# A two-layer decoder trunk on one core: the first layer's normed tokens made from a transposed load instead of from rows and transposes

## The chip, the cores and the metric

The kernel runs on one core of a Trainium2 chip. The metric is device time in microseconds for one execution. A core has engines that run side by side and meet at semaphores: TensorE (PE, with its weight loads shown as PEld), VectorE (DVE), ScalarE (ACT), GpSimd (POOL) and SyncE (SP), whose queue issues nearly all DMAs here. Each engine takes its instructions in the order in which the program holds them, so an instruction that waits holds up everything behind it on that engine.

## The reference

`x` is (1, 512, 1024), `mem` is (1, 256, 1024), all in float32. Cut to what matters:

```python
def rmsnorm(x, g):
    return x * lax.rsqrt(jnp.mean(x * x, axis=-1, keepdims=True) + EPS) * g

def reference(x, mem, norm_g, fox_w_in, fox_b_f, ret_w_in, mem_norm_g, w_mem_kv, w_out, final_norm_g):
    mem_n = rmsnorm(mem, mem_norm_g)
    for i in range(2):
        h = rmsnorm(x, norm_g[i])
        proj = h @ (fox_w_in if i == 0 else ret_w_in)[0]     # q, k, v, (forget logits,) q_mem, z
        main = fox_attention(...) if i == 0 else retention(...)       # 12 heads of 128
        memo = mem_cross_attention(q_mem, mem_n, w_mem_kv[i])         # 4 heads of 128
        x = x + (jnp.concatenate([main, memo], -1) * jax.nn.silu(z)) @ w_out[i]
    return rmsnorm(x, final_norm_g)
```

## The kernel before

Every product is made of three products of fp32r halves: an operand is split into a high part (`H`, a ScalarE cast) and a low part (`L`, the rest, by VectorE), and TensorE adds up H·H, H·L and L·H. Weights come in pieces of 128x1024 (512 KB). A piece is loaded by SP into one of four `raw` buffers, ScalarE casts it to `wH` (L136), VectorE makes `wL` (L137), and there are four buffers of each. When TensorE has used a piece up, `retire` splits the next loaded one and, behind its `wL`, `load_piece` (L118) asks for another. So ScalarE's cast of piece n waits until TensorE is done with piece n-4, and the load of piece n until `wL` of piece n-4 is written.

TensorE's order is written out by hand: `cycle(...)` takes a list of fillers (the projections, which use up pieces) and jobs (norms, attention steps), whose steps are hung between fillers at offsets from the table `OFF`. The orders of VectorE, ScalarE, GpSimd and SP are left to a scheduler that goes by priorities (`due`), except for the first splits, whose own order is fixed.

The program begins so:

- `start_mem` loads the transposed memory `memT` and the first pieces. A VectorE memset of `warm` (L900, a `dd` buffer) is followed on TensorE by 13 products on it (L904), ahead of any that counts.
- Cycle one: `f_vm` (memory values of layer 1, pieces 1 to 4, 48 products of 512 columns; L437, L450), `spread` of the memory's factors (L183), `f_km` four times (memory keys of layer 1, pieces 5 to 8, 24 products of 256 columns each; L60). After each key block VectorE scales the sums (L417), ScalarE casts them and VectorE makes the low part.
- Cycle two: `f_km` four times for layer 0 (pieces 9 to 12), `f_vm` for layer 0 (pieces 13 to 16). Between them hang the four `norm` jobs of layer 0: ScalarE squares a block of 128 rows of x (L192), GpSimd makes the factor (L193, L194), VectorE multiplies by factor and `norm_g` (L195), TensorE transposes it in eight products with the identity (L202), and ScalarE and VectorE split the result into `hH` and `hL` (L157, L158).
- Then layer 0's `f_v` on `hH` and `hL` (pieces 17 and 18, L60 with 268 columns), and all the rest.

Of the kernel before, what the change touches and what calls it, by code (L numbers as in the profile page):

```python
# [16 lines left out]
D = 1024  # L17
S = 512
NMEM = 256
EPS = 1e-6  # L20
# [7 lines left out]
PBASE = 1000  # L28
SPAN5 = 17
SPAN5F = 16  # L30
WARM = 13
MAXK = 1.4
WT = 1088


@with_exitstack
def tile_hybrid(ctx, tc, x_in, mem_in, memT_in, g_cols, norm_g, fin_g, b_f, wv0, wp, index, consts, cosT, sinT, dec, out):
    nc = tc.nc
    P = 128
    KD = D // P  # L40
# [10 lines left out]
    def ps_at(kind, shape, dt, name):  # L51
        tag = TAGS[kind]
        return psum.tile(shape, dt, name=name, tag=tag, bufs=BUFS[tag])
# [21 lines left out]
    def tile_(tag, shape, dt=F32):  # L75
        return work.tile(shape, dt, name=tag, bufs=BUFS[tag])

    csb = cst.tile([P, P], F32, name="csb")
    gc = cst.tile([P, KD], F32, name="gc")
    rbm = cst.tile([P, NMEM], F32, name="rbm")  # L80
    ident = csb[:, 0:P]
    nhalf = cst.tile([P, 1], F32, name="nhalf")
    G.memset(nhalf, -0.5)
    eps_t = cst.tile([P, 1], F32, name="eps_t")
# [14 lines left out]
    def load_g(ap):  # L99
        return load(ap.partition_broadcast(P))  # L100
# [62 lines left out]
    def split_new(tag, src, scale=None):  # L163
        H, L = tile_(tag, [P, 512], F32R), tile_(tag, [P, 512], F32R)
        split_to(H, L, src, scale)
        return H, L
# [236 lines left out]
    def f_km(l, h):  # L403
        key = (l, "km", h)

        def fn():
            H, L = pieces[key]
            mT = st["mT"]
            ps = acc_tile()
            terms = []  # L410
            for w, c in ((H, 0), (H, 1), (L, 0)):
                for k in range(KD):
                    terms.append((w[:, k * P:(k + 1) * P], mT[k][c]))
            mm_group(ps[:, :NMEM], terms)
            kt = tile_("km" if l == 0 else "qk", [P, 2, NMEM], F32R)
            kn = tile_("dd", [P, 512])
            V.tensor_tensor(out=kn[:, :NMEM], in0=ps[:, :NMEM], in1=rbm, op=ALU.mult)  # L417
            split_to(kt[:, 0, :], kt[:, 1, :], kn[:, :NMEM])
            st[l, "km", h] = kt
            retire(key)  # L420
        return [([key], fn)]
# [255 lines left out]
    def g_forget():  # L677
# [44 lines left out]
        forget=(0, 2, 3),  # L722
        norm=(0, 2),
        memr=(0, 2.4),
        xload=(0, 1, 2, 3, 4),
    )
    GEN = dict(mem=g_mem, fox=g_fox, ret=g_ret, retn=g_ret, ret2=g_ret, forget=g_forget, norm=norm_gen, memr=lambda: memr_gen(), xload=lambda: xload_gen())

    cycles = []
    tail_jobs = []  # L730
# [12 lines left out]
    def start_mem():  # L743
        nc.scalar.dma_start(out=gc, in_=g_cols)
        src = [tile_("vv", [P, 4, NMEM]) for _ in range(2)]
        rows = [tile_("vv", [P, D]) for _ in range(2)]
        nc.sync.dma_start(out=src[0], in_=memT_in[0])
        load_piece()
        nc.sync.dma_start(out=src[1], in_=memT_in[1])
        for _ in range(BUFS["raw"] - 1):  # L750
            load_piece()
        nc.sync.dma_start(out=csb, in_=consts[:, 0:P])
        for b in range(2):
            nc.sync.dma_start(out=rows[b], in_=mem_in[b * P:(b + 1) * P, :])
        st["msrc"], st["mrows"] = src, rows
        mT = [[tile_("gg", [P, 2, NMEM], F32R) for _ in range(2)] for _ in range(4)]
        st["mTt"] = mT
        st["mT"] = [(m[0][:, k, :], m[1][:, k, :]) for m in mT for k in range(2)]
# [12 lines left out]
        prep_piece(ends)  # L771

    def memr_gen():
        st["mr"] = [rstd_of(st["mrows"][b], st["mrows"][b], f"mr{b}") for b in range(2)]
        yield
        spread(st["mr"], rbm)
        yield

    def xload_gen():
        st["g", 0] = load_g(norm_g[0])  # L780
        yield
        for t in range(NT):
            nc.sync.dma_start(out=xt[t], in_=x_in[t * P:(t + 1) * P, :])
            yield
    def build_layer(l):
        late = []
        M = "fox" if l == 0 else "ret"
# [11 lines left out]
        for pr in range(6):  # L799
# [26 lines left out]


    cycle(f_vm(1, [[(i, 0), (i, 1)] for i in range(4)], first=True) +
          sum([f_km(1, h) for h in range(4)], []), [("memr", (), 1.5), ("xload", (), 0.5)], mode=8)
    cycle(sum([f_km(0, h) for h in range(4)], []) + f_vm(0, [[(i, 0), (i, 1)] for i in range(4)]),  # L830
          [("norm", (t, ("g", 0)), 2.0 * t) for t in range(NT)], start="x", mode=9)
    build_layer(0)

    cycle(f_out_last(0, (5,), lambda *a: None), [("norm", (t, ("g", 1)), t + 0.5) for t in range(NT)],
# [60 lines left out]
    def emit():  # L895
        lead = ExitStack()
        lead.enter_context(tc.manual_schedule(engines={mybir.EngineType.SP}))
        start_mem()
        warm = tile_("dd", [P, 512], F32R)
        V.memset(warm.bitcast(F32), 0.0)  # L900
        A.activation(small.tile([P, 1], F32, name="ss"), eps_t, AF.Copy, scale=1.0)
        wps = acc_tile()
        for i in range(WARM):
            PE.matmul(wps, lhsT=warm[:, :P], rhs=warm, start=(i == 0), stop=(i == WARM - 1))  # L904
        with tc.manual_schedule(engines={mybir.EngineType.DVE, mybir.EngineType.Pool, mybir.EngineType.Activation}):
            for i in range(4):
                if i:
                    mem_split(2 * i)
                    mem_split(2 * i + 1)
                    prep_piece()  # L910
                else:
                    first_splits()
        carry = []
        for ci, (fillers, jobs, start, mode, last) in enumerate(cycles):
            if start == ("lead", 0):
                spill()
                lead.close()
                tro = tile_("dd", [P, 2 * P])
                tc.keep_in_program_order(nc.sync.dma_start(out=tro, in_=consts[:, P:3 * P]))
                tc.keep_in_program_order(A.copy(out=tri, in_=tro[:, :P]))  # L920
                tc.keep_in_program_order(A.copy(out=ones, in_=tro[:, P:]))
                nc.sync.dma_start(out=bfb, in_=b_f.partition_broadcast(P))
            elif start == "l1":
                st["g", 1] = load_g(norm_g[1])
            elif start == "end":
                st["g", 2] = load_g(fin_g)
                end.enter_context(tc.manual_schedule(engines={mybir.EngineType.DVE, mybir.EngineType.Pool, mybir.EngineType.Activation}))
            elif start == ("lead", 1):
                km_load()
            elif start == ("mem", 1):  # L930
                vm_load()
            nF = len(fillers)
            ev = []
            for kind, args, base in jobs:
                box = {}

                def step(kind=kind, args=args, box=box):
                    if "g" not in box:
                        box["g"] = GEN[kind](*args)
                    with due(now[0] + PRIO[0]):  # L940
                        next(box["g"])
                for off in OFF[kind]:
                    ev.append([base + off, step])
            if ev:
                k = min(MAXK, nF / (mode or max(p for p, _ in ev) + 1))
                for e in ev:
                    e[0] *= k
            if start == "l1":
                ev.append([nF + 1.2, flush_retired])
            ev = sorted(carry + ev, key=lambda e: e[0])  # L950
            for c in range(nF):
                with due(now[0] + PRIO[1]):
                    fillers[c][1]()
                now[0] += 1
                while ev and ev[0][0] < c + 1:
                    ev.pop(0)[1]()
            carry = []
            if last:
                tail_jobs.extend(e[1] for e in ev[-1:])
                for e in ev[:-1]:  # L960
                    e[1]()
            else:
                carry = [[p - nF, f] for p, f in ev]

    end = ExitStack()
    tri = cst.tile([P, P], F32R, name="tri")
    ones = cst.tile([P, P], F32R, name="ones")
    bfb = cst.tile([P, 12], F32, name="bfb")
    engines = {"PE": mybir.EngineType.PE, "ACT": mybir.EngineType.Activation, "DVE": mybir.EngineType.DVE,
               "POOL": mybir.EngineType.Pool}  # L970
# [98 lines left out]
```

## Time and profile before

| | us |
|---|---|
| median of three runs (925.40 to 925.78) | 925.57 |
| the profiled execution itself | 925.52 |
| its span, from the first instruction to the last | 923.7 |

The span is what the views of the profile cover; 1.82 us of the profiled execution lie around it. Busy time of an engine says how much of the span it was at work; of a busy TensorE the ends are modelled, so the start times of its instructions tell more than its share.

### The profile page before, as it was taken

To read this page: it belongs to the slowest core of one execution; us is meant where nothing else is said; L and a number is where in the kernel's file an instruction comes from. 1 tells how busy PE (TensorE), PEld (TensorE's weight loads), DVE (VectorE), ACT (ScalarE), POOL (GpSimd) and SP (SyncE) were. 2 spreads that over 40 slices of the span, in tenths; PEclk is the share of its full clock that TensorE was granted. 3 is DMA by queue.
4 is the path that set the end of the run, shared out by engine and by line. 5 is a ranking of instruction groups with operands and counts; after the bars stand their busy time and mean duration, and the time that the engine had idled before them with its cause. 6 is when DMAs were issued, how large, how long until landed. Compare 5 with 4: busy or idle time off the path is not lost.

```text
span 923.7 us, 12322 instructions
## 1 busy us (share of the span) xinstructions
PE 914.7 (99%) x4623; PEld 778.0 (84%) x4623; DVE 593.5 (64%) x1060; ACT 437.2 (47%) x767; POOL 33.6 (4%) x91
## 2 busy tenths in 40 slices
PE   9999999999999999999999999999999999999997
PEld 7998888888888888888898898888888888888985
DVE  6866664553755564645557756576678675888865
ACT  6744453332544233433325444454457464676642
POOL 0100100000000000000000010000000000000001
PEclk9999999999999999999999999999999999999999
DMA  9774322222332221423223152323323321632302
GB/s 337 265 258 142 116 92 92 90 71 69 127 101 81 78 94 53 144 78 103 81 95 100 46 160 70 109 73 95 111 87 119 114 81 58 182 103 81 115 1 91
DMA packets 32195, 100.69 MB, mean 109 GB/s; under 512 B 4348, under 2 KB 4860, under 8 KB 32136
## 3 DMA queue, kind: packets, MB, share of 16 engines
q1 hardware_dynamic: 30984, 97.55, 32.5%
q0 software_dynamic: 864, 2.10, 0.8%
q8 instruction: 36, 0.59, 0.3%
q10 hardware_dynamic: 288, 0.27, 0.1%
q14 instruction: 23, 0.19, 0.1%
HBM read 92.53 MB, written 4.22 MB: 105 GB/s over the span
## 4 chain that ended last, share of the span: by engine, by line
PE 98%; DMA 1%; issue 0%; DVE 0%; ACT 0%; SPq 0%; POOLq 0%; DVEq 0%; POOL 0%; ACTq 0%
PE acc L226 45%; PE acc L60 23%; PE acc L322 10%; PE s L60 6%; PE o L560 5%; PE acc L379 2%; PE acc L450 2%; PE pt L594 1%; PE o L60 1%; PE acc L385 1%; PE pt L529 1%; PE pt L202 1%; DMA raw<-in_wp_dram 1%; DVE wL L137 0%; ACT wH L136 0%
## 5 line engine op out<-in xcount | busy, mean ns | idle before, releaser
L137 DVE TENSOR_TENSOR wL<-raw,wH 128x1024 fp32r<-128x1024 f32 x148 | 180.8, 1224 | 103.9 <-ACT wH L136 64.0
L136 ACT CAST wH<-raw 128x1024 fp32r<-128x1024 f32 (+1 forms) x147 | 153.5, 1049 | 69.8 <-PE acc L226 34.8
L226 PE MATMUL acc<-hL,wH 128*128 128x512 f32 x608 | 163.6, 394 | 0.0
L226 PE MATMUL acc<-hH,wH 128*128 128x512 f32 x608 | 153.5, 394 | 0.0
L226 PE MATMUL acc<-hH,wL 128*128 128x512 f32 x608 | 150.6, 390 | 0.0
L60 PE MATMUL acc<-wH,gg 128*128 128x512 f32 x416 | 135.8, 393 | 0.0
L226 PEld LDWEIGHTS acc<-hH,wL 128*128 128x128 f32 x608 | 114.1, 188 | 24.5
L226 PEld LDWEIGHTS acc<-hH,wH 128*128 128x128 f32 x608 | 111.0, 188 | 21.3
L226 PEld LDWEIGHTS acc<-hL,wH 128*128 128x128 f32 x608 | 111.3, 188 | 20.6
L60 PEld LDWEIGHTS acc<-wH,gg 128*128 128x128 f32 x416 | 78.1, 188 | 15.6
L60 PE MATMUL acc<-wL,gg 128*128 128x512 f32 x208 | 81.1, 390 | 0.0
L342 DVE TENSOR_TENSOR x<-acc,x 128x512 f32<-128x512 f32 (+1 forms) x73 | 49.7, 681 | 38.2 <-PE acc L60 31.1
L157 ACT CAST pTH<-pt 128x128 fp32r<-128x128 f32 (+2 forms) x64 | 29.8, 467 | 63.2 <-PE pt L594 50.6
L584 ACT ACTIVATE p<-dd,nm 128x128 f32<-128x128 f32 (+3 forms) x48 | 27.0, 563 | 68.0 <-DVE nm L580 67.8
L60 PE MATMUL s<-qk 128*128 128x256 f32 (+3 forms) x240 | 53.5, 326 | 0.0
L322 PE MATMUL acc<-wH,hH 128*128 128x512 f32 x128 | 50.4, 394 | 0.0
L322 PE MATMUL acc<-wH,hL 128*128 128x512 f32 x128 | 49.9, 390 | 0.0
L158 DVE TENSOR_TENSOR pTL<-pt,pTH 128x128 fp32r<-128x128 f32 (+2 forms) x64 | 34.2, 536 | 24.3 <-ACT pTH L157 24.1
L322 PE MATMUL acc<-wL,hH 128*128 128x512 f32 x128 | 49.9, 390 | 0.0
L560 PE MATMUL o<-pTH,vv 128*128 128x512 f32 (+1 forms) x192 | 48.4, 314 | 0.0
L157 ACT CAST gg<-sz 128x512 fp32r<-128x512 f32 x28 | 17.4, 622 | 60.9 <-DVE sz L495 39.9
L60 PEld LDWEIGHTS s<-qk 128*128 128x128 f32 x240 | 40.3, 189 | 6.4 <-DVE p L634 0.3
(197 smaller groups left out, 1354.9 us busy)
## 6 DMA issues: line engine op xcount, KB each, us to landing
raw<-in_wp_dram SPq DMA_DIRECT2D x146, 512.0 KB, 3.6
cbc<-c_d SPq DMA_DIRECT2D x12, 256.0 KB, 3.4
cbc<-in_dec_dram SPq DMA_DIRECT2D x12, 256.0 KB, 3.2
dd<-dd SPq DMA_DIRECT2D x48, 64.0 KB, 2.0
x<-in_x_dram SPq DMA_DIRECT2D x4, 512.0 KB, 6.3
out_dram<-vv SPq DMA_DIRECT2D x3, 512.0 KB, 2.6
raw<-in_wv_dram SPq DMA_DIRECT2D x2, 536.0 KB, 4.2
vv<-in_memT_dram SPq DMA_DIRECT2D x2, 512.0 KB, 4.6
```

Source lines behind the costliest of these rows:

```text
L60: PE.matmul(ps, lhsT=l, rhs=r, start=(i == 0), stop=(i == n - 1))
L136: A.copy(out=H[:, :n], in_=raw[:, :n])
L137: V.tensor_tensor(out=L[:, :n], in0=raw[:, :n], in1=H[:, :n].bitcast(F32), op=ALU.subtract)
L157: A.copy(out=dH, in_=src)
L158: V.tensor_tensor(out=dL, in0=src, in1=dH.bitcast(F32), op=ALU.subtract)
L226: PE.matmul(box["ps"], lhsT=a[:, k * P:(k + 1) * P], rhs=b[:, k, :], start=(n == 0), stop=(n == 23))
L322: PE.matmul(ps, lhsT=a, rhs=b, start=(k == 0 and n == 0), stop=(k == KD - 1 and n == 2))
L342: V.tensor_tensor(out=dst, in0=ps, in1=dst, op=ALU.add)
L379: PE.matmul(ps, lhsT=a, rhs=b, start=(i == 0), stop=False)
L450: PE.matmul(box[b], lhsT=a, rhs=w, start=(i == 0 and n == 0), stop=(i == 3 and n == 5))
L560: PE.matmul(o[:, j * P:], lhsT=a, rhs=b, start=(j == 0 and i == 0), stop=(j == NT - 1 and i == 2))
L584: A.activation(p[:, :n], dd[:, :n], AF.Exp, bias=nm, scale=-1.0, accum_out=sm)
```

## The change

Layer 0's normed tokens are no longer made from rows of x. The host passes x once more, transposed (`xT`, four pieces of 128x2x512), and `h` is made with channels on the partitions and tokens in the columns:

- `xload` loads the four pieces of `xT`; the rows of x, which the residual sum needs later, are loaded by `x_load` at the start of the cycle `("mem", 0)`, as the code stands; the load of `norm_g[0]` as a row is gone, and its columns come with `gc`.
- `xsq` squares the eight halves of `xT` on ScalarE (`p`, two buffers), adds them up in seven GpSimd adds (`sqs`, two buffers), splits the sum, and multiplies both parts by a matrix of ones on TensorE, so that every partition holds each token's sum of squares. ScalarE and VectorE then make the factor (`cbc`), with another activation table than before.
- `h0` makes, for each of the eight halves, `xT * g * factor` on VectorE, and splits it into `hH` and `hL`.
- `ones` is loaded and cast at the start, in a `dd` buffer that is taken ahead of `warm`'s.

```diff
     csb = cst.tile([P, P], F32, name="csb")
-    gc = cst.tile([P, KD], F32, name="gc")
+    gc = cst.tile([P, 2 * KD], F32, name="gc")
...
+    ones = cst.tile([P, P], F32R, name="ones")
...
-        xload=(0, 1, 2, 3, 4),
+        xload=(0, 1, 2, 3),
+        xsq=(0, 1, 2, 3, 4.2, 5.4),
+        h0=(0, 1, 2, 3),
...
         nc.sync.dma_start(out=csb, in_=consts[:, 0:P])
+        st["ones"] = tile_("dd", [P, P])
+        nc.sync.dma_start(out=st["ones"], in_=consts[:, 2 * P:3 * P])
...
     def memr_gen():
+        A.copy(out=ones, in_=st["ones"])
...
     def xload_gen():
-        st["g", 0] = load_g(norm_g[0])
-        yield
+        st["xT"] = []
+        for i in range(4):
+            t = tile_("vv", [P, 2, S])
+            nc.sync.dma_start(out=t, in_=xT_in[i])
+            st["xT"].append(t)
+            yield
+
+    def xsq_gen():
+        acc = None
+        for i in range(4):
+            for u in range(2):
+                sq = tile_("p", [P, 512])
+                A.activation(sq, st["xT"][i][:, u, :], AF.Square)
+                if acc is None:
+                    acc = sq
+                else:
+                    new = tile_("sqs", [P, 512])
+                    G.tensor_tensor(out=new, in0=acc, in1=sq, op=ALU.add)
+                    acc = new
+            yield
+        parts = split_new("dd", acc)
+        yield
+        sb = ps_at("s", [P, 512], F32, name="s")
+        mm_group(sb, [(ones, x) for x in parts])
+        y, t = tile_("cbc", [P, 512]), tile_("cbc", [P, 512])
+        A.activation(y, sb, AF.Abs_reciprocal_sqrt, bias=eps_t, scale=1.0 / D)
+        A.activation(t, y, AF.Square)
+        V.scalar_tensor_tensor(out=t, in0=sb, scalar=D * EPS, in1=t, op0=ALU.add, op1=ALU.mult)
+        V.scalar_tensor_tensor(out=y, in0=t, scalar=-3.0 * D, in1=y, op0=ALU.add, op1=ALU.mult)
+        A.activation(y, y, AF.Copy, scale=-0.5 / D)
+        st["xrb"] = y
+        yield
+
+    def h0_gen():
+        for i in range(4):
+            for u in range(2):
+                k = 2 * i + u
+                hn = tile_("dd", [P, 512])
+                V.scalar_tensor_tensor(out=hn, in0=st["xT"][i][:, u, :], scalar=gc[:, KD + k:KD + k + 1],
+                                       in1=st["xrb"], op0=ALU.mult, op1=ALU.mult)
+                split_to(hH[:, k, :], hL[:, k, :], hn)
+            yield
+
+    def x_load():
         for t in range(NT):
             nc.sync.dma_start(out=xt[t], in_=x_in[t * P:(t + 1) * P, :])
...
-          sum([f_km(1, h) for h in range(4)], []), [("memr", (), 1.5), ("xload", (), 0.5)], mode=8)
+          sum([f_km(1, h) for h in range(4)], []), [("memr", (), 1.5), ("xload", (), 0.5), ("xsq", (), XSQ)], mode=8)
     cycle(sum([f_km(0, h) for h in range(4)], []) + f_vm(0, [[(i, 0), (i, 1)] for i in range(4)]),
-          [("norm", (t, ("g", 0)), 2.0 * t) for t in range(NT)], start="x", mode=9)
+          [("h0", (), H0)], start="x", mode=9)
...
+            elif start == ("mem", 0):
+                x_load()
```

Three places where the change moves instructions. The first is the head of VectorE's queue, before: `dd` is the buffer of the 13 warm-up products, `raw`, `wH`, `wL` are the first pieces, `gg` the split memory.

```order
L900 MEMSET dd 128x512
L131 CAST wH<-raw 128x512 [waits DMAHW2_49]
L769 SCALAR_TENSOR_TENSOR gg<-vv,gc,gg 128x256 [waits DMAHW1_49,DMAHW0_49,Activation_49]
L769 SCALAR_TENSOR_TENSOR gg<-vv,gc,gg 128x256 [waits Activation_49]
L137 TENSOR_TENSOR wL<-raw,wH 128x1024 [waits DVE_49,Activation_49]
L161 SCALAR_TENSOR_TENSOR gg<-vv,gc,gg 128x256 [waits Activation_49] x2
L137 TENSOR_TENSOR wL<-raw,wH 128x1024 [waits DMAHW4_49,Activation_49]
```

The same head of VectorE's queue with the change (L140 is the old L137, L777 the old L769, L951 the old L900):

```order
L134 CAST wH<-raw 128x512 [waits DMAHW2_49]
L777 SCALAR_TENSOR_TENSOR gg<-vv,gc,gg 128x256 [waits DMAHW1_49,DMAHW0_49,Activation_49]
L777 SCALAR_TENSOR_TENSOR gg<-vv,gc,gg 128x256 [waits Activation_49]
L140 TENSOR_TENSOR wL<-raw,wH 128x1024 [waits DVE_49,Activation_49]
L164 SCALAR_TENSOR_TENSOR gg<-vv,gc,gg 128x256 [waits Activation_49] x2
L140 TENSOR_TENSOR wL<-raw,wH 128x1024 [waits DMAHW4_49,Activation_49]
L951 MEMSET dd 128x512
```

The memset stood first; now it stands behind the low part of piece 2. TensorE's first product waits for it in both programs.

The second place is ScalarE around layer 0's first two key blocks, before: `x` are rows of x, `km` the keys, `wH` the pieces 12 and 13.

```order
L136 CAST wH<-raw 128x1024 [waits DMAHW5_49,PE_49,Activation_49]
L192 ACTIVATE vv,ss<-x_84 128x1024 [waits DMAHW6_49]
L157 CAST km<-dd 128x256 [waits DVE_49]
L136 CAST wH<-raw 128x1024 [waits DMAHW7_49,PE_49,Activation_49]
L157 CAST hH<-pt 128x4x128 [waits PE_49] x2
```

There with the change: `p` are squares of `xT` (in `vv`), `sqs` the GpSimd sums, `s` the product with ones, `cbc` the factor; the four `wH` are pieces 12, 13, 14 and 15.

```order
L139 CAST wH<-raw 128x1024 [waits DMAHW2_49,PE_49]
L801 ACTIVATE p<-vv 128x512 [waits DMAHW3_49,Pool_49]
L801 ACTIVATE p<-vv 128x512 [waits Pool_49]
L160 CAST km<-dd 128x256 [waits DVE_49]
L139 CAST wH<-raw 128x1024 [waits DMAHW4_49,PE_49]
L160 CAST dd<-sqs 128x512 [waits Pool_49]
L139 CAST wH<-raw 128x1024 [waits DMAHW5_49,PE_49]
L814 ACT_TABLE_LOAD
L814 ACTIVATE cbc<-s,eps_t 128x512 [waits PE_49]
L160 CAST km<-dd 128x256 [waits DVE_49]
L815 ACTIVATE cbc<-cbc 128x512 [waits Activation_49]
L139 CAST wH<-raw 128x1024 [waits DMAHW6_49,PE_49]
```

Squares that wait for GpSimd, the split of its sum and a table load now stand between the casts of the pieces.

The third place is VectorE ahead of layer 0's `f_v`, before: the 128x1024 `wL` are pieces 14, 15 and 16, the two of 1072 are 17 and 18.

```order
L137 TENSOR_TENSOR wL<-raw,wH 128x1024 [waits DMAHW1_49,Activation_49]
L137 TENSOR_TENSOR wL<-raw,wH 128x1024 [waits DMAHW2_49,Activation_49]
L158 TENSOR_TENSOR km<-dd,km 128x256 [waits Activation_49]
L417 TENSOR_TENSOR dd<-acc,rbm 128x256 [waits PE_49]
L195 SCALAR_TENSOR_TENSOR vv<-x_85,rstd_687,vv 128x1024 [waits DMAHW0_49,Pool_49]
L158 TENSOR_TENSOR hL<-pt,hH 128x4x128 [waits Activation_49] x2
L158 TENSOR_TENSOR km<-dd,km 128x256 [waits Activation_49]
L137 TENSOR_TENSOR wL<-raw,wH 128x1024 [waits DMAHW3_49]
L137 TENSOR_TENSOR wL<-raw,wH 128x1072 [waits DMAHW4_49,Activation_49]
L137 TENSOR_TENSOR wL<-raw,wH 128x1072 [waits DMAHW5_49,Activation_49]
```

There with the change, the end of the pass that makes `h`: L827 is the product `xT * g * factor` into `dd`, of which the first five, with four of the `hL`, stand above these rows, behind the `wL` of piece 15.

```order
L827 SCALAR_TENSOR_TENSOR dd<-vv,gc,cbc 128x512
L827 SCALAR_TENSOR_TENSOR dd<-vv,gc,cbc 128x512 [waits DMAHW3_49,DVE_49]
L161 TENSOR_TENSOR hL<-dd,hH 128x512 [waits Activation_49]
L827 SCALAR_TENSOR_TENSOR dd<-vv,gc,cbc 128x512
L161 TENSOR_TENSOR hL<-dd,hH 128x512 [waits Activation_49]
L161 TENSOR_TENSOR hL<-dd,hH 128x512
L161 TENSOR_TENSOR hL<-dd,hH 128x512 [waits Activation_49]
L140 TENSOR_TENSOR wL<-raw,wH 128x1024 [waits DMAHW7_49]
L140 TENSOR_TENSOR wL<-raw,wH 128x1072 [waits DMAHW0_49,PE_49]
L140 TENSOR_TENSOR wL<-raw,wH 128x1072 [waits DMAHW1_49,PE_49]
```

All eight products and all eight low parts `hL` now stand in one pass ahead of the `wL` of piece 16.

## Rows read from the trace of the kernel before

**Rows 1.** The page, busy time of TensorE: us, share of the span, instructions.

```profile
PE 914.7 (99%) x4623; PEld 778.0 (84%) x4623; DVE 593.5 (64%) x1060; ACT 437.2 (47%) x767; POOL 33.6 (4%) x91
```

**Rows 2.** Waits of TensorE's products: who for whom, us in total, times, longest.

```profile
PE acc L904 <- DVE dd L900: 1.4, 1, 1.4
PE acc L450 <- DVE wL L137: 0.8, 1, 0.8
```

**Rows 3.** Timeline of the start: start us, us, engine, line, operation, tiles.

```profile
0.90 0.48 DVE L900 MEMSET dd<- 128x512 f32 x1 [0.90 <-PEq L1057]
...
1.44 5.42 PE L904 MATMUL acc<-dd 128*128 128x512 f32 x13 [1.44 <-DVE dd L900]
...
6.47 1.79 PEld L437 LDWEIGHTS acc<-wH,gg 128*128 128x128 f32 x8
...
9.51 1.23 DVE L137 TENSOR_TENSOR wL<-raw,wH 128x1024 fp32r<-128x1024 f32 x1 [0.52 <-ACT wH L136]
...
18.63 0.64 PEld L183 LDWEIGHTS pt<-csb,mr 128*128 128x128 f32 x4
...
19.18 1.98 PEld L60 LDWEIGHTS acc<-gg,wH 128*128 128x128 f32 x16
```

**Rows 4.** The chain that ended last, in order of time: start us, us, what.

```profile
19.45 17.28 PE acc L60 x144
...
138.37 5.47 PE acc L226 x24
```

**Rows 5.** Timeline of TensorE's weight loads at the first and last group of transposes.

```profile
36.47 0.90 PEld L202 LDWEIGHTS pt<-csb,vv 128*128 128x128 f32 x8
...
37.33 1.97 PEld L60 LDWEIGHTS acc<-gg,wH 128*128 128x128 f32 x16
...
55.67 1.02 PEld L202 LDWEIGHTS pt<-csb,vv 128*128 128x128 f32 x8
...
56.66 0.19 PEld L60 LDWEIGHTS acc<-wH,hH 128*128 128x128 f32 x1
```

**Rows 6.** Timeline at the end of a key block, and VectorE's work on its sums.

```profile
27.81 1.99 PEld L60 LDWEIGHTS acc<-gg,wH 128*128 128x128 f32 x16
...
28.13 0.42 DVE L417 TENSOR_TENSOR dd<-acc,rbm 128x256 f32<-128x256 f32 x1 [1.26 <-PE acc L60]
```

**Rows 7.** Groups by line and shape: count, busy us, mean ns, idle before.

```profile
L137 DVE TENSOR_TENSOR wL<-raw,wH 128x1024 fp32r<-128x1024 f32 x146 | 178.3, 1223 | 103.6 <-ACT wH L136 63.7 <-PE acc L226 38.4 <-issue 0.6
L158 DVE TENSOR_TENSOR gg<-sz,gg 128x512 fp32r<-128x512 f32 x28 | 19.3, 689 | 8.4 <-ACT gg L157 7.9 <-PE acc L60 0.4
...
L136 ACT CAST wH<-raw 128x1024 fp32r<-128x1024 f32 x145 | 151.4, 1049 | 67.1 <-PE acc L226 34.8 <-issue 14.9 <-PE acc L60 13.6
L157 ACT CAST gg<-sz 128x512 fp32r<-128x512 f32 x28 | 17.4, 622 | 60.9 <-DVE sz L495 39.9 <-PE acc L60 15.2 <-DVE sz L671 5.5
L663 ACT ACTIVATE dd<-s,eps_t 128x512 f32<-128x512 f32 x12 | 8.3, 691 | 2.1 <-PE s L60 2.0
L157 ACT CAST qk<-dd 128x256 fp32r<-128x256 f32 x4 | 1.6, 406 | 5.2 <-DVE dd L417 5.2
```

**Rows 8.** Timeline of ScalarE in layer 1: a change of activation table.

```profile
876.37 1.28 ACT L663 ACT_TABLE_LOAD   x1
877.67 0.69 ACT L663 ACTIVATE dd<-s,eps_t 128x512 f32<-128x512 f32 x1
```

**Rows 9.** Groups by line and shape, GpSimd: its largest operation.

```profile
L575 POOL TENSOR_SCALAR_AFFINE_SELECT dd<-dd 128x128 f32<-128x128 f32 x48 | 16.3, 341 | 369.5 <-DVE dd L574 369.5
```

**Rows 10.** Timeline of GpSimd, and of VectorE beside it.

```profile
30.13 0.19 POOL L193 TENSOR_SCALAR rstd<-ss 128x1 f32<-128x1 f32 x1 [13.95 <-ACT vv L192]
...
41.11 1.21 DVE L137 TENSOR_TENSOR wL<-raw,wH 128x1024 fp32r<-128x1024 f32 x1
...
41.24 1.13 POOL L193 TENSOR_SCALAR rstd<-ss 128x1 f32<-128x1 f32 x1 [4.23 <-ACT vv L192]
```

**Rows 11.** Timeline of VectorE: two low parts of 512 columns in a row.

```profile
39.58 1.27 DVE L158 TENSOR_TENSOR hL<-pt,hH 128x512 fp32r<-128x512 f32 x2
```

**Rows 12.** DMA issues of the first 100 us: KB each, us to landing.

```profile
x<-in_x_dram SPq DMA_DIRECT2D x4, 512.0 KB, 6.3
```

More of the change, by code (lines that the diff above doesn't have):

```diff
@@ L30 @@
 SPAN5F = 16
+XSQ = 4.3
+H0 = 2.6
 WARM = 13
@@ L36, in tile_hybrid @@
 @with_exitstack
-def tile_hybrid(ctx, tc, x_in, mem_in, memT_in, g_cols, norm_g, fin_g, b_f, wv0, wp, index, consts, cosT, sinT, dec, out):
+def tile_hybrid(ctx, tc, x_in, xT_in, mem_in, memT_in, g_cols, norm_g, fin_g, b_f, wv0, wp, index, consts, cosT, sinT, dec, out):
     nc = tc.nc
@@ L724, in tile_hybrid @@
         memr=(0, 2.4),
-        xload=(0, 1, 2, 3, 4),
-    )
-    GEN = dict(mem=g_mem, fox=g_fox, ret=g_ret, retn=g_ret, ret2=g_ret, forget=g_forget, norm=norm_gen, memr=lambda: memr_gen(), xload=lambda: xload_gen())
+        xload=(0, 1, 2, 3),
+        xsq=(0, 1, 2, 3, 4.2, 5.4),
+        h0=(0, 1, 2, 3),
+    )
+    GEN = dict(mem=g_mem, fox=g_fox, ret=g_ret, retn=g_ret, ret2=g_ret, forget=g_forget, norm=norm_gen, memr=lambda: memr_gen(), xload=lambda: xload_gen(),
+               xsq=lambda: xsq_gen(), h0=lambda: h0_gen())
     cycles = []
@@ L917, in emit @@
                 lead.close()
[L918 to L921, printed above, removed]
+                tro = tile_("dd", [P, P])
+                tc.keep_in_program_order(nc.sync.dma_start(out=tro, in_=consts[:, P:2 * P]))
+                tc.keep_in_program_order(A.copy(out=tri, in_=tro))
                 nc.sync.dma_start(out=bfb, in_=b_f.partition_broadcast(P))
+            elif start == ("mem", 0):
+                x_load()
             elif start == "l1":
@@ L966, in tile_hybrid @@
     tri = cst.tile([P, P], F32R, name="tri")
-    ones = cst.tile([P, P], F32R, name="ones")
     bfb = cst.tile([P, 12], F32, name="bfb")
@@ L1050 @@
     xs, ms = np.asarray(x)[0], np.asarray(mem)[0]
+    xT = xs.T.reshape(4, 2, 128, 512).transpose(0, 2, 1, 3)
     memT = ms.T.reshape(2, 4, 128, 256).transpose(0, 2, 1, 3)
-    gcols = np.asarray(mem_norm_g).reshape(8, 128).T
-    ins = [("x", xs), ("mem", ms), ("memT", memT), ("gcols", gcols), ("norm_g", np.asarray(norm_g)),
+    gcols = np.stack([np.asarray(mem_norm_g), np.asarray(norm_g)[0]]).reshape(16, 128).T
+    ins = [("x", xs), ("xT", xT), ("mem", ms), ("memT", memT), ("gcols", gcols), ("norm_g", np.asarray(norm_g)),
            ("final_norm_g", np.asarray(final_norm_g)),
@@ L1063 @@
     o = nc.dram_tensor("out_0_dram", (512, 1024), F32, kind="ExternalOutput").ap()
-    xa, ma, mta, gca, ng, fg, bf, v0, wpa, ca, ct, st, de = aps
+    xa, xta, ma, mta, gca, ng, fg, bf, v0, wpa, ca, ct, st, de = aps
     with tile.TileContext(nc, schedule_with_timeline_sim=TLS) as tc:
-        tile_hybrid(tc, xa, ma, mta, gca, ng, fg, bf, v0, wpa, index, ca, ct, st, de, o)
+        tile_hybrid(tc, xa, xta, ma, mta, gca, ng, fg, bf, v0, wpa, index, ca, ct, st, de, o)
     r = run_bass_kernel_spmd(nc, [arrays], core_ids=[0])
```

## The prediction

> **What bounds the kernel now.** I read the page first. TensorE is busy for 99% of the span [rows 1], and its ends are modelled, so the next view is the one of its waits: in the whole run its products wait twice, 1.4 us for the memset and 0.8 us for a `wL` [rows 2], both within the first 11 us. From there on nothing holds it. In the chain that ended last six key blocks run without a break in 17.28 us, 2.88 us each, and a filler of 24 products of 512 columns takes 5.47 us, 0.228 us a product [rows 4]. So whatever TensorE loses or saves is the time of the run, and whatever another engine does is free until TensorE waits for it. I cost the change against the profiled execution, 925.52 us, which stands 0.05 under the median of the three runs.
>
> **The start.** The memset ran at 0.90 to 1.38, TensorE's first warm-up product began at 1.44, and its first real weight load at 6.47, 5.03 us after [rows 3]. With the change VectorE comes to the memset behind the low part of piece 2, which hangs on loads that the change leaves in place; that ends at 9.51 + 1.23 = 10.74 [rows 3]. Then 0.48 for the memset and 0.06 to the first product give 11.28, and the 13 warm-up products put the first real one at 16.31: 9.84 late. Part of that comes back. Before, the 48 products up to the factor's first weight load took 6.47 to 18.63, 12.16 us [rows 3], where 48 at 0.228 are 10.94; the 1.22 of waiting falls away, since by 16 us the splits are done. Net **+8.62**. The clock is the one thing that may differ here: the granted clock shows 1.00 from the start, but the 13 products came every 0.4 us (5.03 / 13) where later ones come every 0.228. If real products still ran at the slower pace for six more, that is 1 us; if the pace rose earlier, about as much is gained.
>
> **TensorE's own work.** Four groups of eight transposes go. The first takes 36.47 to 37.33, 0.86, the last 55.67 to 56.66, 0.99 [rows 5]; four at the mean are **-3.70**. Two products with ones come, 2 x 0.228 = **+0.46**.
>
> **The product with ones.** TensorE reaches it after 16.31 + 10.94 + 0.55 (the factor's products, 18.63 to 19.18 [rows 3]) + 17.28 = 45.1. Is the sum split by then? I followed the rows of ScalarE, GpSimd and VectorE by hand from the ends of the key blocks (30.6, 33.5, 36.4, 39.3, 42.2), whose sums VectorE can read 0.32 after the next block begins [rows 6], with ScalarE's 1.05 a piece, 0.62 a square or split, 0.41 a key cast, VectorE's 1.22 a `wL` and 0.69 a low part of 512 columns [rows 7]. ScalarE's squares stand between its casts, and a square waits for the add that frees its `p` buffer. What an add costs no row shows. GpSimd's 128 columns take 0.34 [rows 9], and 0.19 is its least with one column [rows 10]; so 512 columns take 0.19 + 4 x 0.15 = 0.79 at least on this engine and 4 x 0.34 = 1.36 at most, with VectorE's 0.69 as the end below. I take 1.1, since two inputs are read. And an add can be held: GpSimd's tiny L193 takes 0.19 alone, but one that began at 41.24, inside a `wL` of VectorE (41.11 to 42.32), took 1.13 and ended with it at 42.37 [rows 10]. So I let a GpSimd read and a VectorE operation with two inputs in SBUF exclude each other, the one that begins first going on.
>
> The adds then start at 33.4, 36.3, 37.4, 40.0, 41.6, 43.9 and 45.4. The last ends at 46.5, its split's high part at 47.2; VectorE's `wL` of piece 13, held until 46.5, ends at 47.7, and the low part at 48.3. The second product starts at 48.4, not 45.3: **+3.1**. Without the exclusion the adds end at 44.9 even at 1.36 each, and what is late is VectorE's own order: key cast to 43.6, piece 13 to 44.6, its `wL` to 45.8, low part 46.4, a wait of 1.2. With it and 1.36 an add the wait is 4.8. [...]
>
> **The pass that makes h.** Counted from the end of the product, E = 48.6, the sum is readable at E + 0.3. ScalarE, late with piece 14, loads the table and makes the root by E + 1.4, casts a key block and squares by E + 2.3; VectorE's two steps end at E + 3.7, its key product and the `wL` of piece 15 at E + 5.3, and the first product of the pass can start. From there VectorE is the bound, for 16 operations of 512 columns, three of 256 and the `wL` of piece 16. Two in a row take 1.27 [rows 11], so about 0.60 each: 16 x 0.60 + 3 x 0.33 + 1.22, with 0.5 of waits for ScalarE (its cast of piece 16, for which TensorE must be done with piece 12, stands ahead of the first `hH`), end at E + 17.7. TensorE wants that `wL` after two key blocks, 36 products and one: 5.76 + 8.2 + 0.23 = E + 14.1. Wait **+3.6**; with 0.69 each and no overlap 5.2. The two pieces behind follow at 1.2 each, in time for `f_v`. A table change costs 1.30 here, with no gap on either side [rows 8].
>
> [...]
>
> **What I cost at nothing.** The rows of x, 2 MB, stand on SP between the loads of pieces 8 and 9, right where TensorE is 9 us late and the pieces are not asked for; piece 9 is asked for at 21.5, lands by 28 even at the slow 6.3 us of x's rows [rows 12], and is cast at 30.7. The `xT` loads stand where x's rows stood. If that cover were missing, each 512 KB ahead of a needed piece would cost at most its 6.3. VectorE loses the row products and ScalarE its row squares, which nothing waited for.
>
> **The sum.** 925.52 + 8.62 - 3.70 + 0.46 + 3.1 + 3.6 = 937.6; half of the missing overlap in the pass makes it **938.0**.
>
> **Rivals.**
> - *Adds without blocking, or cheap ones.* The product waits 1.2 or less: 935.7. For it: one row is thin evidence for adds of 512 columns. Chance 0.2.
> - *Adds at the upper end and blocked.* 939.7 with 1.36, 942 if each add also meets a second `wL`. Chance 0.13.
> - *The pass is ready in time.* VectorE would have to be 3.6 faster; then 934.4, and with an unheld product 932. Against it: 19 operations and a `wL` in a row. Chance 0.07.
> - *Faster.* TensorE has slack later: if it waited somewhere for something that a later start doesn't move, such as a transfer, the losses would be swallowed and the saving of 3.24 left: 922.3. It decides from 12 us of such waits on; the views show 2.2, all before the loss [rows 2]. Chance 0.03.
> - *The losses only just cover the saving*, within 0.2% (1.9 us, about what a measurement of this kernel can tell from no change): that needs 10 us of error on one side. Chance 0.02.
>
> **How the numbers follow.** The forecast (936.5 to 939.5) holds 0.55, the first three rivals 0.40 together, all slower: 0.95 slower, 0.02 same, 0.03 faster. The range reaches over the unheld product, 935.7 less 1.2 for the pace of the start, and the upper end of blocked adds and an unoverlapped pass: 934.5 to 942.
>
> **What would show it.** In the new profile TensorE's first product should start at 11.3 and the first real one near 16.3; the first key block near 27.8; the second product with ones should wait for VectorE's low part, at about 48; GpSimd's adds should differ in length by what VectorE does; the list of waits should name the `wL` of piece 16 with 3 to 5 us; layer 0's `f_v` should start near 69, where it was 56.66. A first product near 1.4 would break the largest term, and a product with ones on time the second.

## The result and the profile after

The changed kernel takes 938.14 us (median of four runs, 937.22 to 938.54) where the kernel before takes 925.67 in the same comparison (four runs, 925.40 to 926.32): a ratio of 1.0132, 95% interval 1.0115 to 1.015. The profiled execution took 938.52, with a span of 936.7.

Busy time of TensorE on the page after, to be held against [rows 1]; then the waits of its products, against [rows 2] (columns as there).

```profile
PE 913.6 (98%) x4593; PEld 776.3 (83%) x4593; DVE 598.7 (64%) x1067; ACT 443.0 (47%) x773; POOL 41.6 (4%) x90
```

```profile
PE acc L955 <- DVE dd L951: 11.3, 1, 11.3
PE acc L453 <- DVE wL L140: 3.3, 1, 3.3
PE s L62 <- ACT dd L160: 1.4, 1, 1.4
PE s L62 <- DVE dd L161: 0.5, 1, 0.5
```

Four waits in place of two, and all four follow from the working above: the memset, the two parts of the sum of squares (the high part makes the first product with ones wait, the low part the second), and the `wL` of piece 16. The rows of weight loads below show the same waits 0.2 to 0.4 longer, since there a wait begins with the end of the last load and not of the last product. The timeline of the start after, against [rows 3] (start us, us, engine, line, operation, tiles):

```profile
9.43 1.23 DVE L140 TENSOR_TENSOR wL<-raw,wH 128x1024 fp32r<-128x1024 f32 x1 [0.50 <-ACT wH L139]
10.71 0.48 DVE L951 MEMSET dd<- 128x512 f32 x1
...
11.25 5.31 PE L955 MATMUL acc<-dd 128*128 128x512 f32 x13 [11.25 <-DVE dd L951]
...
16.18 1.79 PEld L440 LDWEIGHTS acc<-wH,gg 128*128 128x128 f32 x8
...
27.07 0.64 PEld L186 LDWEIGHTS pt<-csb,mr 128*128 128x128 f32 x4
```

The memset stands behind the `wL` of piece 2, and the factor's weight load is at 27.07 where it was at 18.63: 8.44 late. Next, the product with ones: the timeline of GpSimd (adds), VectorE and ScalarE, and TensorE's weight loads.

```profile
32.81 1.31 POOL L806 TENSOR_TENSOR sqs<-p 128x512 f32<-128x512 f32 x1 [16.29 <-ACT p L801]
...
42.33 2.16 POOL L806 TENSOR_TENSOR sqs<-sqs,p 128x512 f32<-128x512 f32 x1
...
44.56 1.33 POOL L806 TENSOR_TENSOR sqs<-sqs,p 128x512 f32<-128x512 f32 x1
...
41.41 1.92 DVE L140 TENSOR_TENSOR wL<-raw,wH 128x1024 fp32r<-128x1024 f32 x1 [0.31 <-ACT wH L139]
...
45.09 1.90 DVE L140 TENSOR_TENSOR wL<-raw,wH 128x1024 fp32r<-128x1024 f32 x1 [0.32 <-ACT wH L139]
46.90 0.68 DVE L161 TENSOR_TENSOR dd<-sqs,dd 128x512 fp32r<-128x512 f32 x1
...
43.94 1.03 PEld L62 LDWEIGHTS acc<-gg,wL 128*128 128x128 f32 x8
46.60 0.19 PEld L62 LDWEIGHTS s<-dd,ones 128*128 128x128 f32 x1 [1.63 <-ACT dd L160]
47.63 0.19 PEld L62 LDWEIGHTS s<-dd,ones 128*128 128x128 f32 x1 [0.85 <-DVE dd L161]
47.74 1.36 PEld L62 LDWEIGHTS acc<-gg,wH 128*128 128x128 f32 x10
```

The add at 32.81, which has VectorE's L420 (33.69) beside it and a `wL` only for its last 0.09 (34.03 to 34.12), takes 1.31. The one at 42.33 takes 2.16: it began inside the `wL` of 41.41, which ended at 43.33, and its own 1.31 counted back from its end (44.49) begin at 43.18. The `wL` of 41.41 and 45.09, which began 0.84 and 0.80 before the end of an add (42.25 and 45.89), take 1.92 and 1.90 where 1.22 is the mean before [rows 7]. The low part of the sum stands behind the second, so the product's second half starts at 47.63. The key block after it begins near 44.90 without the products (43.94 and eight loads of 0.12) and at 47.74 with them: 2.84, of which 0.46 are the two products and 2.4 are wait.

Last, the end of the pass, TensorE's weight loads against the last row of [rows 5], and the windows behind (columns: window, its length, busy us and count of PE, PEld, DVE, ACT, POOL, granted clock, DMA share, GB/s):

```profile
65.57 0.19 PEld L453 LDWEIGHTS acc<-wL,gg 128*128 128x128 f32 x1 [3.71 <-DVE wL L140]
...
68.92 0.33 PEld L62 LDWEIGHTS acc<-wH,hH 128*128 128x128 f32 x1
```

```profile
66.00:67.00 1.00, 1.00 (x6) 0.81 (x5) 1.00 (x2) 0.00 (x0) 0.00 (x0) 0.96 0.44 115
67.00:68.00 1.00, 1.00 (x4) 0.78 (x3) 1.00 (x2) 0.69 (x1) 0.00 (x0) 0.50 1.09 377
...
70.00:71.00 1.00, 1.00 (x8) 1.00 (x8) 0.70 (x1) 1.00 (x3) 0.00 (x0) 0.83 0.99 385
71.00:72.00 1.00, 1.00 (x10) 1.00 (x9) 0.61 (x2) 0.41 (x1) 0.00 (x0) 1.00 0.98 401
```

The wait for `wL` is 3.7. Behind it the granted clock goes from 1.00 to 0.50; if the windows of 0.96 and 0.83 are mixtures of these two, it stays there from about 66.9 to 70.3. In that stretch the products of 512 columns start 0.43 apart (weight loads at 68.49 and 68.92) instead of 0.23, and those of `f_v`, 268 columns, 0.22 apart instead of 0.12. `f_v` starts at 68.92, 12.26 later than in [rows 5]; the span is 13.0 longer.

### The profile page after: what moved, and what is told of

The parts are those of the page before. It is cut to its first block, busy times and chain, and to the rows that moved or that the text cites. A ratio compares the mean times of both kernels' runs of the same rounds, so it can differ in the third digit from the quotient of the medians.

```text
span 936.7 us, 12279 instructions
## 1 busy us (share of the span) xinstructions
PE 913.6 (98%) x4593; PEld 776.3 (83%) x4593; DVE 598.7 (64%) x1067; ACT 443.0 (47%) x773; POOL 41.6 (4%) x90
## 4 chain that ended last, share of the span: by engine, by line
PE 95%; DVE 2%; issue 1%; ACT 1%; POOL 1%; DMA 1%; SPq 0%; POOLq 0%; DVEq 0%; ACTq 0%
PE acc L229 45%; PE acc L62 21%; PE acc L325 9%; PE s L62 6%; PE o L563 5%; PE acc L382 2%; PE pt L597 1%; PE acc L453 1%; PE o L62 1%; PE acc L388 1%; PE pt L532 1%; POOL sqs L806 1%; DMA raw<-in_wp_dram 1%; DVE dd L827 1%; PE acc L955 1%
## 5 line engine op out<-in xcount | busy, mean ns | idle before, releaser
L140 DVE TENSOR_TENSOR wL<-raw,wH 128x1024 fp32r<-128x1024 f32 x148 | 182.2, 1233 | 109.7 <-ACT wH L139 70.3
L161 DVE TENSOR_TENSOR pTL<-pt,pTH 128x128 fp32r<-128x128 f32 (+2 forms) x64 | 34.3, 537 | 24.3 <-ACT pTH L160 24.1
```

Of the source, the lines that this page charges most:

```text
L140: V.tensor_tensor(out=L[:, :n], in0=raw[:, :n], in1=H[:, :n].bitcast(F32), op=ALU.subtract)
L161: V.tensor_tensor(out=dL, in0=src, in1=dH.bitcast(F32), op=ALU.subtract)
```

## The experiments

Two theories of each loss were set against each other, first by undoing one thing at a time, then by putting the repairs together. "Shift" is the start of the factor's weight load, "f_v" that of layer 0's first `f_v` weight load, both from the timelines; before 18.63 and 56.66, after 27.07 and 68.92. All ratios are to the kernel before.

**memset_first.** The memset, and the products on it, move into the block whose order on VectorE is written by hand; so do, behind the first splits, the cast of `ones` and the squares of the memory rows (`memr_gen`), which keeps their places on ScalarE.

```diff
         with tc.manual_schedule(engines={...DVE, ...Pool, ...Activation}):
+            V.memset(warm.bitcast(F32), 0.0)
...
             for i in range(4):
...
+            memr_gen()
```

> VectorE's memset stands first in its row again; all else is the changed kernel. Theory (the late memset costs the 8.44 us by which the first key block moved): first product near 1.4, first real one near 6.5, key block near 19.2, time 938.1 - 8.4 = 929.7, with the waits for the product with ones (2.4) and for wL (3.7) still there. Rival (the late start was what hid the 2 MB of x's rows ahead of piece 9): TensorE waits for a piece between 20 and 30 us, up to 6 us, and the time is 932 to 936. Second rival (the late memset hid behind something else that is late anyway): less than 3 us gained, above 935.

Measured: 935.54 (934.76 to 937.01; 1.0108, 1.0093 to 1.0123). The start came back, shift 18.52, but only 2.6 us of time. The list of TensorE's waits in this kernel says where the rest went, and the windows show the clock:

```profile
PE s L62 <- ACT dd L160: 7.0, 1, 7.0
PE acc L453 <- DVE wL L140: 3.5, 2, 2.7
PE acc L958 <- DVE dd L954: 1.4, 1, 1.4
```

```profile
35.00:40.00 5.00, 2.19 (x19) 1.99 (x17) 3.87 (x5) 3.52 (x7) 4.76 (x4) 1.00 0.78 277
40.00:45.00 5.00, 0.80 (x1) 0.29 (x1) 4.19 (x5) 3.37 (x5) 3.36 (x2) 0.69 0.34 114
45.00:50.00 5.00, 4.82 (x26) 4.72 (x27) 3.40 (x6) 3.65 (x6) 0.00 (x0) 0.63 0.69 220
```

TensorE reaches the key blocks 8.55 us sooner (18.52 against 27.07), and the second half of the product with ones starts only 2.45 sooner, at 45.18. So the late memset had been hiding most of what the sums cost, and the time is the second rival's. The first rival had half of the reason: no piece holds up TensorE between 20 and 30 us, but one holds up ScalarE, whose cast ahead of the first squares waits 6.74 for it.

```profile
27.98 1.05 ACT L139 CAST wH<-raw 128x1024 fp32r<-128x1024 f32 x1 [6.74 <-DMA raw<-in_wp_dram]
```

**memset_first_x_late.** The same, with each load of x's rows held to its place in the program's order, which puts the four far behind the start.

```diff
-            nc.sync.dma_start(out=xt[t], in_=x_in[...])
+            tc.keep_in_program_order(nc.sync.dma_start(out=xt[t], in_=x_in[...]))
```

> As memset_first, and x's rows are loaded after the whole of layer 0's first three cycles, far behind the start. Theory: x's rows cost nothing at the start in either, so the same 929.7 within 1. Rival (the rows compete with the pieces and with xT once the start is early): 1 to 6 us below memset_first. The squares can start earlier if xT lands earlier; if so the wait for the product with ones shrinks by up to 2.4.

Measured: 934.50 (932.76 to 936.02; 1.0095, 1.008 to 1.011). GpSimd's first add begins at 24.79 instead of 30.47, and the product's second half at 42.09 instead of 45.18, so the rows of x do delay the squares once the start is early: between 19 and 65 us no cast on ScalarE waits for a load, and the first square, at 22.71, waits 2.99 for its own `xT` load. In time the two can't be told apart: what the product gains, the clock takes (0.56 from 40 to 45 us and 0.61 from 60 to 65, where memset_first has 0.69 and 1.00), and f_v is at 66.24 against 66.52. The wait for the product is now split, 2.4 and 1.9, and the six later adds run back to back for 10.99, 1.83 from one to the next: three of them take 2.16 to 2.23, with VectorE's `wL` (1.95 to 1.98) and key low parts (1.51 and 1.52) beside them.

**wl_ahead_of_pass.** The changed kernel, in which the splits of pieces 16 and 17 get the first priority.

```diff
-            with due(first_use.get(order[min(nprep[0], len(order) - 1)], 0) + PRIO[2]):
+            with due(0 if nprep[0] in (15, 16) else first_use.get(...) + PRIO[2]):
```

> The changed kernel; the splits of pieces 16 and 17 get a high priority, so that VectorE does their wL inside the pass that makes h and not behind it. Theory (the 3.7 us wait is VectorE's order, and the slower clock after it, 1.6 us, hangs on the wait): the wait at piece 16 goes, the clock stays at 1.00, f_v waits up to 1.5 for the end of the pass: 933 to 934.5. Rival (VectorE's sum of work is the bound, and the wait only moves to f_v): 937 to 938.

Measured: 934.99 (934.92 to 935.19; 1.0101, 1.0084 to 1.0118), f_v at 64.78, clock 1.00 in every window up to 80 us. The `wL` of pieces 16 and 17 now run at 55.18 and 59.17, inside the pass, and the wait for piece 16 is gone from the list; what is left is a wait inside `f_v` for piece 18's `wL`:

```profile
PE acc L62 <- DVE wL L140: 0.9, 1, 0.9
```

3.15 less by moving two VectorE instructions: of the 3.7, all but about 1 was an order and not a lack of VectorE time. The time is half a microsecond above what was expected; in the profiled execution (934.93) 0.36 of that is a later start (shift 27.43).

**products_in_the_wait.** The changed kernel with work for TensorE in its longest wait.

```diff
+                        if l == 0 and (i, b, n) == (3, 0, 1):
+                            fill = ps_at("s", [P, 512], F32, name="s")
+                            for j in range(15):
+                                PE.matmul(fill, lhsT=a, rhs=w, start=(j == 0), stop=(j == 14))
```

> The changed kernel with 15 products more (3.4 us at 0.228), whose result nothing reads, between the first product of piece 16 and its wait for wL. Theory (TensorE's idle time of 3.7 us is what lets the granted clock fall to 0.50): the clock stays at 1.00 from 66 to 71, products at 0.228, time 938.1 - 1.6 = 936.5. Rival (the clock falls there for another reason): rows at 0.43 again, time 938.1 or a little above.

Measured: 936.97 (936.23 to 937.47; 1.0121, 1.0106 to 1.0136). Its windows over the stretch in which the changed kernel ran at 0.50:

```profile
67.00:68.00 1.00, 1.00 (x8) 0.92 (x7) 1.00 (x2) 0.36 (x1) 0.00 (x0) 1.00 1.07 270
68.00:69.00 1.00, 1.00 (x10) 1.00 (x9) 1.00 (x3) 1.00 (x3) 0.00 (x0) 1.00 0.70 246
```

The clock stays at 1.00 where it was 0.50. The shift is 26.29 here, 0.78 less than after, nearly all of it by the pace of the 13 products; the span is 2.3 less, which leaves 1.5 for the clock. The medians differ by 1.2, with that pace in both.

**adds_left_out.** The changed kernel without the adds: `acc = sq` in place of them, so that only the last square is split and summed.

> The changed kernel without GpSimd's seven adds: only the last square is split and summed, so h has another factor. Theory (the wait for the product with ones comes from the adds, their length and the VectorE reads that they hold): VectorE's wL are back at 1.22 and its key low parts at 0.42, the wait of 1.9 falls to 0.5 or less, the wait for wL of piece 16 stays near 3.7: 936 to 936.8. Rival (VectorE's own order is what is late): the wait stays above 1.2 and the time above 937.

Measured: 936.33 (935.77 to 936.93; 1.0114, 1.0097 to 1.0131). No wait for the product with ones is left, VectorE's `wL` there are back at 1.22 and 1.23 and its key low parts at 0.42 and 0.43, the wait for the `wL` of piece 16 is 3.5, and the clock falls behind it as before (0.50 from 65 to 68 us).

```profile
41.92 1.23 DVE L140 TENSOR_TENSOR wL<-raw,wH 128x1024 fp32r<-128x1024 f32 x1 [0.52 <-ACT wH L139]
45.43 1.22 DVE L140 TENSOR_TENSOR wL<-raw,wH 128x1024 fp32r<-128x1024 f32 x1 [0.26 <-ACT wH L139]
```

f_v is at 66.78 with a shift of 27.59: 2.14 + 0.52 = 2.66 less than after, for a wait of 2.4 and a little of the other. VectorE's order moved too (the sum's low part now ahead of a `wL`), so the run shows what the adds and their place cost together.

**x_late_wl_ahead.** memset_first_x_late and wl_ahead_of_pass in one.

> memset_first_x_late with the splits of pieces 16 and 17 ahead, adds on GpSimd as in the changed kernel. Theory (wL wait and the clock after it are the same two terms as in the changed kernel): 934.5 - 2.7 - 1.6 + 0.9 = 931.1, the waits for the product with ones (2.4 and 1.9) and the slow clock after them still there. Rival (the end of the pass is the bound now): the wait moves to f_v, above 933.

Measured: 930.21 (929.68 to 930.92; 1.0049, 1.0034 to 1.0064), f_v at 60.60. The waits for the product are 2.4 and 1.6, and the clock is 0.50 from 40 to 45 us, from the first of them on. What is left above the kernel before is mainly the wait for the sum of squares and the slower clock behind it.

**squares_to_product.** No adds: ScalarE's squares go to TensorE, rounded to the products' type. This stands on memset_first_x_late, and three more things move with it: pieces 14 to 17 are split ahead, the `xT` loads go together, and the sum and the pass get earlier places.

```diff
+            parts.append([tile_(tag, [P, 512], F32R) for tag in ("p", "sqs")])
+            for u in range(2):
+                A.activation(parts[i][u], st["xT"][i][:, u, :], AF.Square)
+            if i:
+                products(i - 1)          # two PE.matmul(sb, lhsT=ones, rhs=...)
-XSQ = 4.3
-H0 = 2.6
+XSQ = 3.3
+H0 = 1.9
```

> memset_first_x_late with pieces 14 to 17 split ahead, the four xT loads together ahead of piece 10, and no adds at all: ScalarE writes the squares in the matmul's type (rounded, without a low part) and TensorE multiplies all eight with ones behind key blocks 2 to 5... the pairs as they come, 8 x 0.228 = 1.82. Theory (the adds and their place are what makes the product late, and with the sum three key blocks earlier the pass is done when f_v starts): no wait over 1 us after the start, clock 1.00, time 925.5 - 3.70 + 1.82 = 923.6, up to 925 with small waits. Rival (VectorE's work up to f_v is the bound even then): f_v waits 2 to 4, time 926 to 929.

Measured: 925.48 (925.24 to 925.81; 0.9998, 0.9989 to 1.0008): all of the loss is gone, nothing is won. TensorE waits 1.0 for the first square and 0.4 at piece 2, the clock is at 1.00, f_v at 56.17 with no wait. The last two products with ones stand behind the fourth key block where they stood behind the sixth, two blocks earlier and not the three of the expectation. The time is above the theory's range and below the rival's. Against what the terms give for f_v (56.66 - 3.70 + 1.82 = 54.8) it is 1.4 late, which is the first pair of squares:

```profile
23.13 0.19 PEld L804 LDWEIGHTS s<-p,ones 128*128 128x128 f32 x1 [1.18 <-ACT p L808]
23.65 0.19 PEld L804 LDWEIGHTS s<-sqs,ones 128*128 128x128 f32 x1 [0.33 <-ACT sqs L808]
```

Another half microsecond comes behind the start of f_v (867.5 from there to the end of the span, 867.0 in the kernel before). xt_early and xt_early_memset_late have it too, and no row explains it. Since several things moved at once, the run shows that the loss can be undone and not what each move is worth.

**pairs_to_product.** VectorE adds the squares of a pair.

> As squares_to_product, but VectorE adds the two squares of a pair (four adds of 0.69, rounded as they are written), so that TensorE makes four products with ones. Theory: 0.91 less on TensorE, 922.7 if VectorE has the 2.8 us to spare. Rival (VectorE is full in the key blocks): its wL come late, and the time is that of squares_to_product or up to 3 us above.

Measured: 926.29 (925.67 to 927.51; 1.0009, 1.0000 to 1.0018). The first product with ones waits 2.2 for its add, since the pair's second square ends only at 24.0: the rival's result by another cause.

**xt_early, xt_early_pairs, xt_early_memset_late.** Three of the four `xT` loads go ahead of piece 8's load; with the squares as they are, with pairs, and with the squares as they are and the memset back behind the `wL` of piece 2.

```diff
+                    if i == 3:
+                        xT_load(range(3))
                     prep_piece()
```

> squares_to_product with three of the four xT loads one place earlier, ahead of piece 8's load, so that the first squares are ready when their product with ones comes. Theory (its only loss against 923.6 are the 0.98 us at the first product with ones, whose xT landed at 22.4, and small waits): that wait goes, 924.3 to 924.8. Rival (DMA is full until 30 us, so pieces 8 and 9 come late in return): a wait of 1 to 3 us for a wL in the key blocks, 925.5 to 927.

> xt_early with VectorE adding the squares in pairs (four products with ones in place of eight). Theory: 0.91 below xt_early, 923.4 to 923.9, since VectorE is idle between 20 and 24 us and can take the first adds there. Rival (2.8 us more on VectorE push the end of the pass past f_v): f_v waits 1 to 2, time 924.5 to 926.

> xt_early with the memset where the changed kernel has it, behind the wL of piece 2; every other row of VectorE and ScalarE stands as in xt_early. Theory (alone, the late memset costs the 8.44 us by which it moved the first key block, and memset_first gained less only because the sums weren't ready): xt_early + 8.4, about 933. Rival (the late start is paid back later): less than 6 us above xt_early.

Measured: 925.94 (925.78 to 926.19; 1.0004, 0.9996 to 1.0013), 924.52 (924.38 to 925.01; 0.999, 0.9981 to 0.9998) and 932.25 (932.14 to 932.54; 1.0072, 1.0057 to 1.0088). The first has a new wait, by its list of waits:

```profile
PE acc L62 <- DVE pTL L164: 1.7, 1, 1.7
PE acc L958 <- DVE dd L954: 1.4, 1, 1.4
PE acc L453 <- DVE wL L140: 0.7, 1, 0.7
```

The early squares stand on ScalarE ahead of the splits of the memory values (L163), and TensorE needs the accumulators that these hold; the time is the rival's, by a cause that neither theory had. The second is above its theory too: 0.6 of the wait for `pTL` is left, and `f_v` is held up by 0.3 and not by the rival's 1 to 2. The third kernel differs from the first by the memset's place alone. Their first factor's weight loads, the first kernel's and then the third's, and their first of f_v:

```profile
18.50 0.64 PEld L186 LDWEIGHTS pt<-csb,mr 128*128 128x128 f32 x4
...
56.64 0.19 PEld L62 LDWEIGHTS acc<-wH,hH 128*128 128x128 f32 x1
```

```profile
27.12 0.64 PEld L186 LDWEIGHTS pt<-csb,mr 128*128 128x128 f32 x4
...
63.29 0.19 PEld L62 LDWEIGHTS acc<-wH,hH 128*128 128x128 f32 x1
```

8.62 late at the first, 6.65 at the second: the late kernel has no wait for `pTL` and none at piece 2. The medians are 6.31 apart, between the rival's 6 and the theory's 8.4: the late start costs its whole length less the waits that it covers.

**pairs_behind_pth.** xt_early_pairs, with the first two squares held behind the splits of the memory values.

> xt_early_pairs with ScalarE's first two squares kept behind its splits of the memory values (L163), for whose low parts TensorE waited 0.6 there. Theory (TensorE's accumulators are held because the squares stand ahead): that wait goes, 923.9 to 924.2. Rival (the squares are then late for their product with ones): a wait of up to 2 there, 924.5 to 926.

Measured: 924.65 (924.41 to 924.98; 0.999, 0.9981 to 0.9999). The wait for `pTL` (0.6) went, one of 0.4 for the second pair's sum came, f_v is at 54.64 against 55.04: no difference that can be measured. That the squares' place made the wait for `pTL` is shown by its going; the time stays in the rival's range. These two are the best versions, 0.1% under the kernel before, with VectorE rounding the sum of each pair.

## Why the prediction was right, point by point

**The start** (predicted +8.62): 8.44. The memset took its place behind the `wL` of piece 2, and the 1.22 of early waiting fell away as said. As an account of the run the term is right. As the price of that place it isn't: taking it back was worth 2.6 us in the changed kernel and 6.3 where the sums were ready.

**The product with ones** (+3.1): 2.4. This was mis-sized, and in two ways that partly cancel. An add takes 1.31 alone, not 1.1, but the first began 0.6 earlier than laid out and only two of the seven were held for long (1.74 and 2.16), so the last ended at 45.89 and not at 46.5, and the low part began at 46.90 and not 47.7. That an add and a `wL` or low part of VectorE hold each other up was seen in these rows: the `wL` that began at 41.41 ended 1.22 after 42.11, about when the add before it was done (42.25), the add of 42.33 in turn ended its own 1.31 after 43.18, about when that `wL` was done (43.33), and three key low parts (L161, 0.42 without an add) that began inside adds took 0.92, 0.64 and 0.63. With the adds out every such row is back at its own length (1.22 and 1.23, 0.42 and 0.43). VectorE's L420, which reads the sums in `acc`, took 0.41 and 0.42 beside adds. That two inputs in SBUF decide it was the author's assumption; no run varied it.

**The pass** (+3.6, and half of a missing overlap, +0.4): 3.7. The first multiply began at 53.15, 5.3 after the product's end at 47.9, as laid out, and the `wL` of piece 16 was ready at 65.5, 17.6 after it where 17.7 was said. From start to start a multiply took 0.66 and a low part 0.60, so the overlap was mostly there and the 0.4 was not needed. (Added up as they stand, the prediction's figures give 17.6 and 14.2, a wait of 3.4; and half of the 1.6 between its 3.6 and its 5.2 would have been 0.8, not 0.4.) The table change took the 1.30 of [rows 8]: ScalarE's cast ended at 47.49, the table load ran from 47.51 to 48.79, and the root began at 48.81.

**The clock** was the step that the prediction left out: it spoke of the pace of the start, not of the clock behind a wait, here 0.50. From the late `wL` to `f_v` went 3.35 (65.57 to 68.92), where it is 2.42 with the wait filled (64.79 to 67.21), and from the start of `f_v` to the end of the span 0.7 more than before (936.7 - 68.92 against 923.7 - 56.66): 1.6 together.

**The sum**: 8.44 - 3.70 + 0.46 + 2.4 + 3.7 + 1.6 = 12.9 on the profiled execution's 925.52, 938.4, against 938.52. So 938.0 was near for a mixed reason: the large terms were right, and that the rest summed to so little was luck. The product's wait was 0.7 too long, the overlap 0.4 and the start 0.2 too much, which together nearly made up for the 1.6 that the clock took.

**What was costed at nothing**: the rows of x cost the changed kernel nothing that shows. Between 11 and 46 us no cast and no square on its ScalarE waits for a load, and TensorE's list names no piece but 16. That the late start is what covers them is borne out by the adds, which with an early start begin 5.7 us sooner when the rows are moved away (24.79 against 30.47). What the rows would have cost in time stays open, 935.54 and 934.50 with ranges that overlap.

**The rivals.** That the adds are cheap fell, by 1.31 and the held rows. Adds at the upper end and blocked had the length nearly (1.31 against 1.36) but not the wait, 2.4 where it had 4.8, since only two adds were held for long. That the pass is ready in time fell in this kernel, but not for want of VectorE time: with two splits moved it was. The rival of slack later in the run fell too: f_v starts 12.26 late and the span ends 13.0 late, with the clock's 0.7 between them; and at 13.0 the losses do far more than cover the saving.

## What to carry to other kernels

The terms of a sum add up along one chain, but the price of undoing one doesn't follow from it: a late start covers every producer behind it that doesn't move with it, so look at what each wait hangs on before calling an offset a cost. A wait on an engine with much to do can be an order: here two splits moved into a pass were worth 3.15 us. Where adds on an otherwise idle engine come late, the engine that needs the sum may make it itself: with the squares taken to TensorE, and their loads and places moved with them, the time fell from 930.21 to 925.48. And look at the clock behind a wait: here the wait of 3.7 us cost another 1.6, with TensorE at a granted 0.50 behind it.

## What the runs showed of the hardware

- The granted clock fell with some waits of TensorE and not with others; lengths and times of it are estimates from the windows, taken as mixtures of 1.00 and 0.50. With the waits of 3.7 us (the changed kernel) and 3.5 (adds_left_out) for the `wL` it went to 0.50, for 3.4 and 3.2 us (products of 512 columns every 0.43 in the first); in memset_first it fell at about 42, inside the wait of 7.0, which ended at 44.15, and was back at 48.7. With the wait of 3.7 filled with products it stayed at 1.00. The waits of 1.6 and 0.9 in the changed kernel left it there, those of 2.4 and 1.9 in memset_first_x_late did not (0.56 from 40 to 45 us). A wait of 2.7 went both ways: no fall in memset_first, 0.61 in memset_first_x_late.
- From the first of the 13 products on `warm` to the first real weight load it took between 4.23 us (11.18 to 15.41 in products_in_the_wait) and 5.29 (1.44 to 6.73 in xt_early_pairs), with 5.03 before and 4.93 after. The changed kernel, wl_ahead_of_pass (5.22) and products_in_the_wait are the same program up to there, so the program alone doesn't set it in these runs, and differences under a microsecond are read between two marks in the trace and not from single times. One execution of each kernel was traced; how often it falls which way is not shown.
- What differs is when the pace changes; the 0.4 of the prediction is a mean of two. In the changed kernel the early ones of these products start 0.43 apart (11.85, 12.27, 12.70), as at a granted 0.50 further on, the last two 0.25 (weight loads at 15.69 and 15.94), near the 0.23 at 1.00, and the change comes at 15.7 us in the changed kernel and at 14.1 in products_in_the_wait. The windows from 14 to 15 us, the changed kernel's first, show it in their counts of products (4 and 6). Their clock says 1.00 in both, so here only the pace shows the difference.

```profile
14.00:15.00 1.00, 1.00 (x4) 0.81 (x3) 0.93 (x1) 1.00 (x4) 0.75 (x1) 1.00 1.04 414
14.00:15.00 1.00, 1.00 (x6) 0.83 (x5) 0.85 (x1) 1.00 (x3) 0.76 (x2) 1.00 1.01 401
```
